# Scaling softmax weights on GpSimd instead of VectorE, with later score and value products, in a two-layer decoder trunk

## The chip, the core and the metric

The kernel runs on one core of a Trainium2 chip. The metric is device time in microseconds of one execution. Engines are named as in the profile: PE is TensorE (matrix products and transposes), PEld its weight loads, DVE is VectorE, ACT is ScalarE, POOL is GpSimd, SP issues the weight transfers. L946 is line 946 of the kernel before.

## The reference

The input is 256 tokens of width 1024 and a memory of 256 rows. Two layers follow each other; each is a half-step SwiGLU feed-forward, a token mixer, and another half-step feed-forward. The mixer of layer 0 is a chunked matrix memory (mLSTM), that of layer 1 is sliding-window attention with 16 heads of 64 channels in 2 groups, a learned sink per head, normalised queries and keys, and a partial rotation. Beside both stand four heads of 128 channels that attend to the memory (the cross heads). Both attentions end in the same way:

```
m = max(s, [sink]);  p = exp(s - m);  denom = sum(p) [+ exp(sink - m)]
out = (p / denom) @ v
```

The division p / denom is the "scaling of the softmax weights" in the title. All is float32.

## The kernel before

**Products.** A float32 product with a weight is made of three products of rounded parts: weights and activations are each split in a high and a low part (`split`, L211 on ACT rounds, L212 on DVE subtracts), and `mm3` (L225 to L227) adds high x high, high x low and low x high. A weight tile of 512 KB feeds 24 matrix products; SP fetches it, and eight split tiles of each part can be held. The small attention products are plain float32: `mmf` (L231) and `transpose` (L236).

**Order of the work.** PE and SP run in the order in which the program is written. That order is made by the class `Weave`. Its main line is the stream of projections, which yields after every four `mm3`, that is twelve matrix products. Beside it live chains, the steps of norms and heads. Each product adds a planned cost to a clock `wv.now`: 0.328 for an `mm3`, 0.107 for a transpose, 0.466 for a 256-column `mmf`; the scores of one window head add 0.97 in all. A chain yields a delay from the table `LAT` and is due when the clock has passed it. At each yield of the main line all chains that are due run one step, the oldest chain first. So a larger delay in `LAT` puts a PE step behind more projection work. The other engines take their instructions as dependencies and the compiler's ordering allow; each works in order.

**A cross head** (`cross_spawn`, L568 on). For each of two groups the query rows are normalised (`head_norm`, L368 on; its power of -1/2 at L379 is on POOL, and L381 and L383 on DVE use it), then transposed on PE (`queries`), copied by ACT with a gain, and two heads start: `cross_s` after this step, the second one `cross_m` later. A head makes scores (L231) into a bank of PSUM, DVE takes the maximum (L591), ACT the exponentials with their sums (L132 is the helper that issues them), DVE the reciprocal (L595) and the scaling (L596). After `cross_p` PE transposes the weights, ACT copies them (L603), after `cross_o` PE multiplies with the values. Cross heads 0 and 1 are those of the first group, 2 and 3 of the second.

**A window head** (`head` in `mixer_b`, L910 on; eight steps, each for two heads of the reference, numbered 0 to 7 here). Queries are normalised, rotated (`rope`, L857 to L860 on DVE), transposed and copied (ACT, out of `gcut`); the two steps of a group start `head` and `head` + `head_m` after that. A step adds a mask by a product (L920), makes scores (L925), DVE takes maxima (L929, L930) and joins the sinks (L932, L933), ACT makes exponentials, DVE sums and inverts (L941, L942) and scales in four instructions (L946): two of 128 columns, two of 256. After `head_p` PE transposes (six transposes), ACT copies (L954), after `head_o` PE multiplies with the values (L961).

The cross heads of layer 0 lie in `mixer_a`, those of layer 1 and the window heads in `mixer_b`. POOL runs the powers of the norms (L251, L379) and a few small transfers in the first feed-forward, and nothing else. Eight banks of PSUM serve all.

Of the kernel before, what the change touches and what calls it, by code (L numbers as in the profile page):

```python
# [15 lines left out]
ALU = mybir.AluOpType  # L16
# [3 lines left out]
P = 128  # L20
T = 256
# [11 lines left out]
def constants():  # L33
# [16 lines left out]

LAT = dict(pieces=1, norm=7.5, norm_b=4.8, mnorm=2.4, x0=16.0, x0_b=7.5, mkeys=7.2, cross=9.5, cross_s=1.5,
           cross_m=3.7, cross_p=8.7, cross_o=3.0, gates=20.0, scores=2.2, scores_m=8.4, num=6.9, num_r=7.5,
           keys=5.5, keys_d=7.2, query=9.0, head=1.5, head_m=2.5, head_p=9.3, head_o=4.0)


WARM = 18
# [40 lines left out]
def tile_trunk(ctx: ExitStack, tc: tile.TileContext, a, out):  # L99
    nc = tc.nc  # L100
# [27 lines left out]
    tt = nc.vector.tensor_tensor  # L128
# [21 lines left out]
    def mo():  # L150
        return mk(pb8, [P, 512], F32, "bank")
# [51 lines left out]
    pieces = [1]  # L203
# [57 lines left out]
    class Norm:  # L261
# [30 lines left out]

        def chain(self, gap=LAT['norm_b']):
            pc = mo()
# [103 lines left out]
    x0 = Norm(G_F1)  # L398

    def memory():  # L400
# [27 lines left out]
        for gi in range(2):  # L428
# [13 lines left out]
            norm.fold()  # L442
            wv.spawn(norm.chain(), LAT['mnorm'])
            gv = Group(wkv, 512, mh, ml, rows=True)
# [123 lines left out]
    def cross_spawn(gr, gi, layer, hsc, ys):  # L568
        qn = unit(F32)
        head_norm(qn, gr.ps, 2, hsc)  # L570
        cell = []

        def queries():
            ps = turn(qn)
            qT = unit(F32)
            act(qT, ps, AF.Copy, scale=gqk[:, layer:layer + 1])
            cell.append(qT)
            for m in range(2):
                wv.spawn(head(m), LAT['cross_s'] + LAT['cross_m'] * m)
            return  # L580
            yield

        def head(m):
            hd, qT = gi * 2 + m, cell[0]
            hi, lo = ys.tiles(4 + gi)
            s = mo()
            for h in range(2):
                mmf(s[:, h * T:(h + 1) * T], qT[:, m, h * P:(h + 1) * P], kT[gi][:, m], T)
            sv = halves(s)
            c = col()  # L590
            nc.vector.tensor_reduce(out=c[:, 2:4], in_=sv, axis=AX.X, op=ALU.max, negate=True)  # L591
            p = unit(F32)
            for h in range(2):
                act(p[:, h], sv[:, h], AF.Exp, bias=c[:, 2 + h:3 + h], accum_out=c[:, 4 + h:5 + h])
            nc.vector.reciprocal(c[:, 6:8], c[:, 4:6])  # L595
            tt(out=p, in0=p, in1=c[:, 6:8].unsqueeze(2).to_broadcast([P, 2, T]), op=ALU.mult)  # L596
            yield LAT['cross_p']
            tps = mo()
            for mc in range(2):
                for h in range(2):  # L600
                    transpose(tps[:, mc * T + h * P:mc * T + (h + 1) * P], p[:, h, mc * P:(mc + 1) * P])
            pT = tmp()
            nc.scalar.copy(pT, halves(tps))  # L603
            yield LAT['cross_o']
            o = mo()
            for mc in range(2):
                mmf(o[:, :T], vM[:, mc, hd * P:(hd + 1) * P], pT[:, mc], T, mc == 0, mc == 1)
            split_plain(o[:, :T], hi[:, m], lo[:, m])
            ys.done.add(8 + hd)

        wv.spawn(queries(), LAT['cross'])
# [251 lines left out]
    def mixer_b(x, nxt):  # L863
# [46 lines left out]
        def head(ch, qr):  # L910
            while wv.now < st.get("at", 1e9):
                yield 1.0
            kd, vr = st["kd"], st["vr"]
            m, j = ch % 2, ch // 4
            hi, lo = ys.tiles(ch // 2)
            c, d = col(), col()
            es = [slice(e * 64, (e + 1) * 64) for e in range(2)]
            sc = [mo(), mo()]
            for s in sc:
                nc.tensor.matmul(s[:, :384], identb, maskb[:, :384], start=True, stop=False, skip_group_check=True)  # L920
                wv.now += 0.16

            for cs, qs, ks in ((slice(0, P), slice(0, P), slice(0, P)), (slice(P, 384), slice(P, T), slice(0, T))):
                for e in range(2):
                    nc.tensor.matmul(sc[e][:, cs], qr[es[e], m, qs], kd[es[e], j, ks], start=False, stop=True,  # L925
                                     skip_group_check=True)
                wv.now += (cs.stop - cs.start) * 0.0017
            for e, s in enumerate(sc):
                nc.vector.tensor_reduce(out=c[:, e:e + 1], in_=s[:, :P], axis=AX.X, op=ALU.max, negate=True)  # L929
                nc.vector.tensor_reduce(out=c[:, 2 + e:3 + e], in_=s[:, P:384], axis=AX.X, op=ALU.max, negate=True)  # L930
            snk = nsink[:, 2 * ch:2 * ch + 2].unsqueeze(1).to_broadcast([P, 2, 2])
            tt(out=v22(c[:, 8:12]), in0=v22(c[:, 0:4]), in1=snk, op=ALU.min)  # L932
            tt(out=v22(c[:, 12:16]), in0=v22(c[:, 8:12]), in1=snk, op=ALU.subtract)  # L933
            p = [unit(F32).rearrange("p a b -> p (a b)") for _ in range(2)]
            for e in range(2):
                for h, cs in ((0, slice(0, P)), (1, slice(P, 384))):
                    i = 2 * h + e
                    act(p[e][:, cs], sc[e][:, cs], AF.Exp, bias=c[:, 8 + i:9 + i],
                        accum_out=d[:, 4 + i:5 + i])
            act(d[:, 0:4], c[:, 12:16], AF.Exp)  # L940
            tt(out=d[:, 8:12], in0=d[:, 0:4], in1=d[:, 4:8], op=ALU.add)  # L941
            nc.vector.reciprocal(d[:, 12:16], d[:, 8:12])  # L942
            for e in range(2):
                for h, cs in ((0, slice(0, P)), (1, slice(P, 384))):
                    i = 2 * h + e
                    nc.vector.tensor_scalar(p[e][:, cs], p[e][:, cs], d[:, 12 + i:13 + i], None, op0=ALU.mult)  # L946
            yield LAT['head_p']
            pTs = []
            for e in range(2):
                tps = mo()  # L950
                for i in range(3):
                    transpose(tps[:, i * P:(i + 1) * P], p[e][:, i * P:(i + 1) * P])
                pT = tmp().rearrange("p a b -> p (a b)")
                nc.scalar.copy(pT[:, :384], tps[:, :384])  # L954
                pTs.append(pT)
            yield LAT['head_o']
            o = mo()
            js = slice(j * 64, (j + 1) * 64)
            for i, cs, src in ((0, slice(0, T), slice(0, T)), (1, slice(P, T), slice(T, 384))):
                for e in range(2):  # L960
                    nc.tensor.matmul(o[es[e], cs], vr[:, i, js], pTs[e][:, src], start=i == 0, stop=i == 1,  # L961
                                     skip_group_check=True)
                wv.now += (cs.stop - cs.start) * 0.0017
            split_plain(o[:, :T], hi[:, m], lo[:, m])
            ys.done.add(ch)
# [61 lines left out]
```

## Time and profile before

| what | value |
|---|---|
| median of 3 runs | 1012.32 us (1012.27 to 1013.65) |
| the profiled execution | 1012.23 us |
| its span, first to last instruction | 1010.4 us |
| granted TensorE clock, mean | 1.000 |
| moved from memory | 180.32 MB read, 180 GB/s over the span |

The rows in the next sections are read like this. In the page's first part: engine, busy us, share of the span, number of instructions. In the chain that ended last: the share of the span in which each engine was what the end waited for. In a row of waits: who waited, for whom, us in total, how often, the longest. In a row of the timeline: start, duration (us), engine, line, operation, output<-inputs, shapes, count of like instructions drawn together, and in brackets the idle time before it and what ended that. In a row of a group: count, then busy us, mean ns of one, idle us before. In a row of stretches: bounds, length, then busy us and count for PE, PEld, DVE, ACT, POOL, then granted clock, share of the transfer engines, GB/s. Ends of matrix products are modelled, since they are pipelined: a product is shown longer than the distance to the next one.

### The profile page before, as it was taken

To read this page: it belongs to the slowest core of one execution; us is meant where nothing else is said; L and a number is where in the kernel's file an instruction comes from. 1 tells how busy PE (TensorE), PEld (TensorE's weight loads), DVE (VectorE), ACT (ScalarE), POOL (GpSimd) and SP (SyncE) were. 2 spreads that over 40 slices of the span, in tenths; PEclk is the share of its full clock that TensorE was granted. 3 is DMA by queue.
4 is the path that set the end of the run, shared out by engine and by line. 5 is a ranking of instruction groups with operands and counts; after the bars stand their busy time and mean duration, and the time that the engine had idled before them with its cause. 6 is when DMAs were issued, how large, how long until landed. Compare 5 with 4: busy or idle time off the path is not lost.

```text
span 1010.4 us, 20624 instructions
## 1 busy us (share of the span) xinstructions
PE 998.5 (99%) x8594; PEld 980.2 (97%) x8594; DVE 655.5 (65%) x1063; ACT 519.5 (51%) x764; POOL 35.7 (4%) x32
## 2 busy tenths in 40 slices
PE   8999999999999999999999999999999999999998
PEld 7999999999999999999999999999987899999998
DVE  6866665577856676665558666656787766666551
ACT  7754445446656554444445544544557754454440
POOL 1200000000001000000000000000121000000000
PEclk9999999999999999999999999999999999999999
DMA  9776656666644566665676666567541347666550
GB/s 308 242 245 200 192 180 185 199 183 179 184 139 133 167 210 195 200 189 170 192 206 205 189 191 201 173 197 198 182 131 66 100 131 220 198 189 185 188 170 21
DMA packets 173204, 182.70 MB, mean 181 GB/s; under 512 B 7124, under 2 KB 168328, under 8 KB 173112
## 3 DMA queue, kind: packets, MB, share of 16 engines
q1 hardware_dynamic: 171872, 179.60, 58.3%
q10 hardware_dynamic: 1016, 1.58, 0.5%
q8 instruction: 67, 1.10, 0.5%
q0 software_dynamic: 224, 0.22, 0.2%
q14 instruction: 25, 0.20, 0.1%
HBM read 180.32 MB, written 1.05 MB: 180 GB/s over the span
## 4 chain that ended last, share of the span: by engine, by line
PE 94%; DVE 3%; ACT 1%; DMA 1%; POOL 0%; issue 0%; SPq 0%; ACTq 0%
PE bank L225 30%; PE bank L226 30%; PE bank L227 30%; PE bank L231 2%; PE bank L236 1%; ACT u L132 1%; DVE wl L212 1%; DMA wr<-in_mem_w_kv_dram 1%; PE bank L961 1%; POOL col L379 0%; DVE col L930 0%; DVE u L383 0%; DVE col L591 0%; PE bank L925 0%; DVE u L946 0%
## 5 line engine op out<-in xcount | busy, mean ns | idle before, releaser
L212 DVE TENSOR_TENSOR wl<-wr,wh 128x1024 fp32r<-128x1024 f32 (+1 forms) x347 | 414.7, 1196 | 279.8 <-ACT wh L211 279.0
L211 ACT CAST wh<-wr 128x1024 fp32r<-128x1024 f32 (+1 forms) x347 | 356.8, 1031 | 393.1 <-PE bank L226 368.9
L225 PE MATMUL bank<-xh,wh 128*128 128x256 f32 x1544 | 429.1, 278 | 0.0
L226 PE MATMUL bank<-xl,wh 128*128 128x256 f32 x1544 | 426.8, 276 | 0.0
L227 PE MATMUL bank<-xh,wl 128*128 128x256 f32 x1544 | 426.8, 276 | 0.0
L226 PEld LDWEIGHTS bank<-xl,wh 128*128 128x128 f32 x1544 | 290.3, 188 | 0.1
L225 PEld LDWEIGHTS bank<-xh,wh 128*128 128x128 f32 x1544 | 290.0, 188 | 0.1
L227 PEld LDWEIGHTS bank<-xh,wl 128*128 128x128 f32 x1544 | 289.9, 188 | 0.0
L225 PE MATMUL bank<-u,wh 128*128 128x256 f32 x896 | 249.3, 278 | 0.0
L226 PE MATMUL bank<-u,wh 128*128 128x256 f32 x896 | 247.6, 276 | 0.0
L227 PE MATMUL bank<-u,wl 128*128 128x256 f32 x896 | 247.6, 276 | 0.0
L225 PEld LDWEIGHTS bank<-u,wh 128*128 128x128 f32 x896 | 168.2, 188 | 1.9 <-issue 1.7
L226 PEld LDWEIGHTS bank<-u,wh 128*128 128x128 f32 x896 | 168.4, 188 | 0.1
L227 PEld LDWEIGHTS bank<-u,wl 128*128 128x128 f32 x896 | 168.3, 188 | 0.0
L225 PE MATMUL bank<-wh,xh 128*128 128x256 f32 x208 | 59.7, 287 | 0.0
L226 PE MATMUL bank<-wl,xh 128*128 128x256 f32 x208 | 57.9, 278 | 0.0
L227 PE MATMUL bank<-wh,xl 128*128 128x256 f32 x208 | 57.9, 278 | 0.0
L476 DVE TENSOR_TENSOR t<-bank,rb 128x256 f32<-128x256 f32 x88 | 36.6, 420 | 7.3 <-PE bank L227 7.3
L225 PEld LDWEIGHTS bank<-wh,xh 128*128 128x128 f32 x208 | 39.1, 188 | 0.5 <-issue 0.3
L226 PEld LDWEIGHTS bank<-wl,xh 128*128 128x128 f32 x208 | 39.1, 188 | 0.1
L227 PEld LDWEIGHTS bank<-wh,xl 128*128 128x128 f32 x208 | 39.0, 187 | 0.0
L479 DVE TENSOR_TENSOR t<-t,bank 128x256 f32<-128x256 f32 x88 | 32.7, 412 | 1.8 <-ACT t L132 1.8
(171 smaller groups left out, 657.5 us busy)
## 6 DMA issues: line engine op xcount, KB each, us to landing
wr<-in_ffn_w_in_dram SPq DMA_DIRECT2D x176, 512.0 KB, 3.6
wr<-in_ffn_w_out_dram SPq DMA_DIRECT2D x80, 512.0 KB, 3.5
wr<-in_a_w_in_dram SPq DMA_DIRECT2D x28, 512.0 KB, 3.9
wr<-in_b_w_in_dram SPq DMA_DIRECT2D x14, 512.0 KB, 4.6
wr<-in_a_w_out_dram SPq DMA_DIRECT2D x12, 512.0 KB, 3.3
wr<-in_b_w_out_dram SPq DMA_DIRECT2D x12, 512.0 KB, 3.4
wr<-in_ffn_w_out_dram SPq DMA_DIRECT2D x16, 256.0 KB, 2.8
wr<-in_mem_w_kv_dram SPq DMA_DIRECT2D x7, 512.0 KB, 8.0
```

Source lines behind the costliest of these rows:

```text
L132: ins = nc.scalar.activation(*args, **kw)
L211: last[0] = nc.scalar.copy(hi[:, i * n:(i + 1) * n], src[:, i * n:(i + 1) * n])
L212: tt(out=lo[:, i * n:(i + 1) * n], in0=src[:, i * n:(i + 1) * n], in1=hi[:, i * n:(i + 1) * n].bitcast(F32), op=ALU.subtract)
L225: nc.tensor.matmul(ps, wh, xh, start=start, stop=False, skip_group_check=True)
L226: nc.tensor.matmul(ps, wh, xl, start=False, stop=False, skip_group_check=True)
L227: nc.tensor.matmul(ps, wl, xh, start=False, stop=stop, skip_group_check=True)
L231: nc.tensor.matmul(ps, lhsT, rhs, start=start, stop=stop, skip_group_check=True)
L236: nc.tensor.transpose(ps, src, ident[:k, :k])
L476: tt(out=t[:, m], in0=ps[m][:, :T], in1=x.rb, op=ALU.mult)
L479: tt(out=t[:, m], in0=t[:, m], in1=ps[m][:, T:], op=ALU.mult)
L961: nc.tensor.matmul(o[es[e], cs], vr[:, i, js], pTs[e][:, src], start=i == 0, stop=i == 1, skip_group_check=True)
```

## The change

The scaling of cross heads, one DVE instruction on 512 columns with the reciprocals broadcast, becomes two POOL instructions on 256 columns, each with its reciprocal as a column. The four scaling instructions of a window head keep their form and go from DVE to POOL. Three delays grow: `cross_s` from 1.5 to 2.5, `cross_o` from 3.0 to 3.5, `head` from 1.5 to 2.5.

```diff
-LAT = dict(pieces=1, norm=7.5, norm_b=4.8, mnorm=2.4, x0=16.0, x0_b=7.5, mkeys=7.2, cross=9.5, cross_s=1.5,
-           cross_m=3.7, cross_p=8.7, cross_o=3.0, gates=20.0, scores=2.2, scores_m=8.4, num=6.9, num_r=7.5,
-           keys=5.5, keys_d=7.2, query=9.0, head=1.5, head_m=2.5, head_p=9.3, head_o=4.0)
+LAT = dict(pieces=1, norm=7.5, norm_b=4.8, mnorm=2.4, x0=16.0, x0_b=7.5, mkeys=7.2, cross=9.5, cross_s=2.5,
+           cross_m=3.7, cross_p=8.7, cross_o=3.5, gates=20.0, scores=2.2, scores_m=8.4, num=6.9, num_r=7.5,
+           keys=5.5, keys_d=7.2, query=9.0, head=2.5, head_m=2.5, head_p=9.3, head_o=4.0)
...
-            tt(out=p, in0=p, in1=c[:, 6:8].unsqueeze(2).to_broadcast([P, 2, T]), op=ALU.mult)
+            for h in range(2):
+                nc.gpsimd.tensor_scalar(p[:, h], p[:, h], c[:, 6 + h:7 + h], None, op0=ALU.mult)
             yield LAT['cross_p']
...
-                    nc.vector.tensor_scalar(p[e][:, cs], p[e][:, cs], d[:, 12 + i:13 + i], None, op0=ALU.mult)
+                    nc.gpsimd.tensor_scalar(p[e][:, cs], p[e][:, cs], d[:, 12 + i:13 + i], None, op0=ALU.mult)
             yield LAT['head_p']
```

## Prediction

> **What bounds the kernel now.** I began with the page: busy time of each engine, then the chain that ended last.
>
> ```profile
> span 1010.4 us, 20624 instructions
> ...
> PE 998.5 (99%) x8594; PEld 980.2 (97%) x8594; DVE 655.5 (65%) x1063; ACT 519.5 (51%) x764; POOL 35.7 (4%) x32
> ...
> PE 94%; DVE 3%; ACT 1%; DMA 1%; POOL 0%; issue 0%; SPq 0%; ACTq 0%
> ```
>
> TensorE (PE) is the bound and holds 94% of the chain; only what makes it idle can be won. GpSimd (POOL) is nearly free. The table of stretches shows where PE idles around the change: the first mixer, a stretch of pure feed-forward, and the second mixer.
>
> ```profile
> 230.00:358.00 128.00, 128.00 (x1060) 125.99 (x1059) 88.85 (x167) 76.88 (x136) 7.03 (x6) 1.00 0.53 158
> 358.00:545.00 187.00, 187.00 (x1648) 187.00 (x1648) 119.43 (x172) 89.79 (x108) 2.24 (x2) 1.00 0.65 197
> ...
> 720.00:840.00 120.00, 114.67 (x942) 103.78 (x942) 88.50 (x235) 72.74 (x176) 15.35 (x9) 1.00 0.39 121
> ```
>
> The first number after the length is PE's busy time. The first mixer loses nothing, the second loses 5.3 us. The second row also gives the pace: 187.00/1648 = 0.1135 us a matmul, so the twelve between two yields of a projection, a "slot" below, are 1.36 us. PE's waits in the second mixer:
>
> ```profile
> PE bank L231 <- ACT u L132: 1.5, 1, 1.5
> PE bank L925 <- ACT u L132: 1.4, 1, 1.4
> PE bank L231 <- ACT t L603: 1.1, 1, 1.1
> PE bank L920 <- DVE u L383: 0.7, 1, 0.7
> PE bank L961 <- ACT u L132: 0.4, 1, 0.4
> PE bank L920 <- ACT t L954: 0.2, 1, 0.2
> ```
>
> They add up to 5.3 us, the whole loss, and are all that this change can give back. The first three lie before 762 us; the timeline shows them with what released them:
>
> ```profile
> 741.74 0.69 ACT L132 ACTIVATE u<-bank,gqk 128x512 f32<-128x512 f32 x1
> ...
> 742.47 0.73 PEld L231 LDWEIGHTS bank<-kT,u 128*128 128x128 f32 x4 [1.66 <-ACT u L132]
> 742.47 1.13 PE L231 MATMUL bank<-kT,u 128*128 128x256 f32 x4 [1.45 <-ACT u L132]
> ...
> 750.45 0.57 ACT L603 COPY t<-bank 128x512 f32<-128x512 f32 x1
> ...
> 751.08 1.13 PE L231 MATMUL bank<-t,vM 128*128 128x256 f32 x4 [1.05 <-ACT t L603]
> ...
> 754.23 0.93 PE L925 MATMUL bank<-u,u 64*128 64x128 f32 x8
> ...
> 760.29 0.74 ACT L132 ACTIVATE u<-bank,gcut 128x512 f32<-128x512 f32 x1
> ...
> 761.09 0.93 PE L925 MATMUL bank<-u,u 64*128 64x128 f32 x8 [1.40 <-ACT u L132]
> ```
>
> Each time PE reaches a score or value product before ScalarE has made its copy: scores of cross head 2, values of cross head 0, scores of window head 2. These are just the three kinds whose delays grow: cross_s, cross_o, head.
>
> **The delays.** The planner runs due chains at yields; a slot is 4 x 0.328 = 1.31 of its time. Set its clock to 0 at the end of the first cross turn. Now: two slots 2.62, scores 0 end 3.56, a slot 4.87, second turn 5.30, scores 1 (due 1.5 + 3.7 = 5.2) end 6.23, a slot 7.54, scores 2 (due 5.30 + 1.5 = 6.8). After: scores 1 are due at 6.2, so a slot comes first (6.61), end 7.54, a slot 8.85, scores 2 (due 7.8). Between second turn and scores 2 stand two slots for one: 1.36 us of work inside a 1.45 us wait. Gain **1.35 us**.
>
> Values of cross head 0: due 3.0 after their transposes, met today after scores 3 (0.93), a slot and the next transposes (0.43), 2.67. After, 3.5 is not met before scores of window head 0, which then stand due and go first (0.97 planned). From the end of scores 3 the copy took until 751.02. The same distance is then covered by about 1.3 us of products for 0.6 us of transposes, and VectorE comes earlier to the max that ScalarE's queue waited for. I take 0.85 of the 1.05 us as gone, from 0 to all.
>
> Window head 2: by the same clock its scores start 4.03 after the end of head 1's scores today and 5.77 after; the difference is 1.74 planned, over a slot. Today the copy ended 761.03 - 755.16 = 5.9 us after those scores, and PE came there 1.40 too early. With 1.7 us more work it comes late enough. Gain **1.40 us**.
>
> The price is that window head 0's scores come nearer to their own copy:
>
> ```profile
> 746.27 1.04 PE L236 MATMUL bank<-con,u 128*128 128x128 f32 x8
> ...
> 747.72 0.71 ACT L132 ACTIVATE u<-bank,gcut 128x512 f32<-128x512 f32 x1
> ```
>
> The copy ended 2.15 us after its transposes began; after, 0.43 + 0.43 + 0.93 + 1.31 = 3.1 us of work stand between, but with one slot fewer ahead of the turn. I take 0.1 us of new wait, at most 0.6. No chain issues a DMA and the projections keep their order, so SP's queue is untouched; POOL's DMAs all lie in the first feed-forward.
>
> **The scaling.** VectorE's cost in this stretch, by group:
>
> ```profile
> L946 DVE TENSOR_SCALAR u<-u,col 128x128 f32<-128x128 f32 (+1 forms) x32 | 8.0, 315 | 0.1
> ...
> L596 DVE TENSOR_TENSOR u<-u,col 128x512 f32<-128x512 f32 x4 | 2.7, 687 | 0.1
> ```
>
> So 10.7 us leave VectorE: 8.0/8 = 1.0 a window head, 0.69 a cross head. VectorE does not bound, so this counts only where it feeds ScalarE ahead of a PE wait: it is the help counted at the second wait. The same instructions on POOL are nowhere in the trace. The nearest rows are its powers:
>
> ```profile
> 727.76 1.01 POOL L379 TENSOR_TENSOR col<-col,mhalf 128x4 f32<-128x4 f32 x1 [4.19 <-DVE col L377]
> ...
> 771.96 2.48 POOL L379 TENSOR_TENSOR col<-col,mhalf 128x8 f32<-128x8 f32 x1 [20.88 <-DVE col L377]
> 779.09 1.64 POOL L379 TENSOR_TENSOR col<-col,mhalf 128x8 f32<-128x8 f32 x1 [4.66 <-DVE col L377]
> ```
>
> Four columns 1.01, eight 1.64: 0.16 a column on a fixed 0.38. The lower end is VectorE's own 0.32 an instruction, the upper 2.48, a power's longest here. I take the fixed part and 1 ns a column (VectorE's 687 ns for 512, rounded up): 0.51 and 0.64, an estimate, so **2.3 us a window head**, 1.3 a cross head, nearer the lower end because a multiplication is what VectorE does there.
>
> The 2.48 stands against 1.64 for the same shape. What else ran:
>
> ```profile
> 771.72 1.22 DVE L212 TENSOR_TENSOR wl<-wr,wh 128x1024 fp32r<-128x1024 f32 x1
> ```
>
> The long power started inside VectorE's weight split and ended 1.50 us after it; a wait of 0.84 is to be reckoned with. Beside this: the Trainium skill, "SBUF — State Buffer", section "Who interferes with whom", says that a VectorE instruction with two SBUF inputs and a GpSimd instruction that reads SBUF exclude each other for a whole instruction, whichever starts second waiting. The trace agrees for POOL's side (2.48 against 1.64); VectorE's waiting side no row here shows. By that rule VectorE would not be relieved of all 10.7 us: that is the second rival.
>
> A window head's weights are thus ready 2.3 - 1.0 + 0.84 = 2.1 us later. The cover is PE's distance to their transposes:
>
> ```profile
> 742.23 0.68 DVE L596 TENSOR_TENSOR u<-u,col 128x512 f32<-128x512 f32 x1
> ...
> 745.27 0.68 DVE L596 TENSOR_TENSOR u<-u,col 128x512 f32<-128x512 f32 x1
> ...
> 749.43 0.60 PE L236 MATMUL bank<-con,u 128*128 128x128 f32 x4
> ...
> 758.93 1.01 DVE L946 TENSOR_SCALAR u<-u,col 128x128 f32<-128x128 f32 x4
> ...
> 788.33 1.01 DVE L946 TENSOR_SCALAR u<-u,col 128x128 f32<-128x128 f32 x4
> ...
> 793.17 0.88 PE L236 MATMUL bank<-con,u 128*128 128x128 f32 x6
> ...
> 806.66 0.82 PE L236 MATMUL bank<-con,u 128*128 128x128 f32 x6
> ```
>
> Window head 4 has 793.17 - 789.34 = 3.8 us, cross head 1 749.43 - 745.95 = 3.5, cross head 0 about 3.8 to the second half of the eight at 746.27, of which the lifted first wait takes 1.4. Each is more than its 2.1 or 1.5. In the first mixer the cover is larger:
>
> ```profile
> 264.00 0.69 DVE L596 TENSOR_TENSOR u<-u,col 128x512 f32<-128x512 f32 x1
> ...
> 270.11 0.60 PE L236 MATMUL bank<-con,u 128*128 128x128 f32 x4
> ```
>
> The new wait is POOL's on the reciprocal. Queued behind it stand the next head's weights and the next query norm's power, which VectorE's line 381 needs. The one that matters follows window head 3:
>
> ```profile
> 769.82 1.01 DVE L946 TENSOR_SCALAR u<-u,col 128x128 f32<-128x128 f32 x4
> ...
> 777.20 0.60 PE L236 MATMUL bank<-con,u 128*128 128x128 f32 x4
> ```
>
> With 2.3 us POOL is done by 772.1, when the power would run anyway (771.96); the turn at 777.20 then stays. For this and for changed bank reuse I add 0.3 us. The three later waits (1.3 us) I leave.
>
> **Sum:** -1.35 - 0.85 - 1.40 + 0.1 + 0.3 = -3.2 us on the profiled execution's own 1012.23 us (span 1010.4 and 1.8 outside it, untouched): 1009.0. The median is 0.09 above that execution, so I forecast **1009.1 us**.
>
> **The rivals.** *POOL too slow (slower).* Place: transposes of the window weights. Head 0's weights begin at 758.93; 32 instructions of p us and two powers (4.1) must end by 806.66 plus the 3.6 us lifted, so p = (51.3 - 4.1)/32 = 1.48 us is where the gain is used up; window head 4 by itself makes PE wait from (793.17 - 788.33)/4 = 1.2. Powers of 1.01 to 2.48 speak for it, the small fixed part of 0.38 against. At p = 1.6 it adds 0.12 x 32 = 3.9 us: **1016.2 us**; at 2.48, 1044.
>
> *The waits only move (same).* VectorE is held up by POOL as POOL is by it, so maxima and copies come no earlier, and waits two and three reappear a slot later. Only the first wait's 1.35 goes, less 0.3 to 0.6: **1011.4 us**. For it: the 0.84 above. Against: cover of 1.7 planned at the third wait needs no help from VectorE.
>
> *All six go (faster).* VectorE, rid of 1.0 us a head, serves the three later waits earlier too. PE's rows understate a wait a little (its weight load has 1.66 where the product has 1.45); with 0.1 for each of six it is 1012.3 - 5.3 - 0.6 = **1006.4 us**.
>
> *It does nothing:* excluded for the order, by the clock above.
>
> **Chances.** Forecast 0.50, all six go 0.10, only moved 0.22, POOL too slow 0.18. A measurement of this kernel can tell about 0.2%, 2 us, from no change: faster is below 1010.3, same up to 1014.3. Of the forecast's half, 0.05 ends above 1010.3. So faster 0.55, same 0.27, slower 0.18. The range runs from 1006.2 (all waits gone, nothing paid) to 1014.8 (p just past 1.48), leaving out most of the slow rival.
>
> As to line rate: the Trainium skill, "GPSIMD Engine Reference", section 4.1, puts one-input work on GpSimd at roughly VectorE's line rate. No run here shows it yet; by it the weights would be no later at all and the sum 0.3 us lower, 1008.8.
>
> **What would show it.** Right: waits at 742 and 761 gone, the one at 751 under 0.3; POOL's multiplications near 0.5 to 0.7 us, longer beside the split of weights; no PE wait on POOL. Wrong: transposes (L236) waiting for POOL; VectorE's splits longer than 1.22 us; new waits on ScalarE's copies a slot later; or the power after window head 3 later than 774.4 and its turn with it.

## The result and the profile after

The changed kernel takes **1016.27 us** (median of 6 runs, 1016.01 to 1017.73; the kernel before on the same chip 1012.3), a ratio of 1.004 with the 95% interval [1.0027, 1.0053]. It is slower by 4 us, where 3.2 us less were forecast, and lies above the range. The profiled execution took 1016.08 us. Two lines of its page (span, and the shares of the chain that ended last), then the rows of the two mixers from the table of stretches. Each stretch runs from PE's last sums of squares ahead of a mixer (the rows L231 `bank<-ones,acc`) to the next ones behind it, so that it can be laid over the same stretch of another kernel; the columns are those of the earlier table.

```profile
span 1014.3 us, 20676 instructions
...
PE 92%; DVE 3%; POOL 2%; ACT 2%; issue 1%; DMA 1%; SPq 0%; POOLq 0%; ACTq 0%; DVEq 0%
```

The same two mixers before:

```profile
223.81:357.75 133.94, 133.94 (x1110) 131.93 (x1109) 91.63 (x172) 78.86 (x137) 7.75 (x7) 1.00 0.55 162
719.04:833.89 114.85, 109.52 (x898) 98.63 (x897) 85.08 (x234) 71.40 (x175) 13.82 (x8) 1.00 0.37 113
```

And after:

```profile
223.64:358.20 134.56, 134.22 (x1110) 131.85 (x1109) 89.49 (x168) 78.87 (x137) 15.11 (x15) 1.00 0.54 161
719.48:837.79 118.31, 110.28 (x899) 98.54 (x898) 76.39 (x198) 71.26 (x175) 48.32 (x48) 1.00 0.35 110
```

VectorE is indeed relieved, by 8.7 us in the second mixer (85.08 to 76.39), GpSimd has 34.5 us more, and GpSimd, nowhere before, holds 2% of the chain. The first mixer is 0.62 us longer, the second 3.46; PE's idle time in the second grew from 5.3 to 8.0, and the other 0.8 us is PE longer busy (109.52 to 110.28). The sum of 4.1 is the whole loss: outside the two stretches both executions spend 737.0 us between PE's very first sums of squares and the end. These first sums stand at 24.3 to 24.7 us in most traces and at 25.9 to 26.2 in four (e2, e12, e14 and e16 below); in just these four the granted clock was 0.50 for 3.4 us between 13 and 18 us. Such executions take some 1.6 us longer (1013.8 for 1012.1, the kernel before), so the experiments below are read by the lengths of these two stretches first, called A (before 133.95, after 134.56) and B (before 114.86, after 118.30). Both come from one profiled execution of each kernel; a second trace of the changed kernel gives 134.56 and 118.20.

PE's waits in the second mixer, after:

```profile
PE bank L921 <- DVE u L383: 2.5, 2, 1.3
PE bank L236 <- POOL u L947: 1.6, 1, 1.6
PE bank L225 <- DVE u L383: 1.1, 1, 1.1
PE bank L231 <- ACT u L132: 1.0, 1, 1.0
PE bank L926 <- ACT u L132: 1.0, 2, 0.7
PE bank L236 <- DVE u L861: 0.4, 1, 0.4
PE bank L231 <- ACT t L604: 0.4, 1, 0.4
```

Hardly a row of before is left: 8.0 us of waits, other ones. The three that the change was to lift are lifted, as the timeline of after shows at the same three products (lines behind 596 have moved by one: L925 is now L926):

```profile
742.94 1.13 PE L231 MATMUL bank<-kT,u 128*128 128x256 f32 x4
...
749.25 0.93 PE L926 MATMUL bank<-u,u 64*128 64x128 f32 x8 [0.31 <-ACT u L132]
750.11 1.13 PE L231 MATMUL bank<-t,vM 128*128 128x256 f32 x4
...
762.49 0.93 PE L926 MATMUL bank<-u,u 64*128 64x128 f32 x8
```

Scores of cross head 2, values of cross head 0 and scores of window head 2 have no wait behind them; window head 0's scores have 0.31, inside the forecast bound of 0.6. So the 3.9 us were won, and 3.9 + 4.1 = 8.0 lost elsewhere. (That the waits left in the second mixer also come to 8.0 is chance: some of these stood there before, and the first mixer and PE's longer busy time are in the other sum.)

**GpSimd's price.** Its groups on the whole kernel:

```profile
L597 POOL TENSOR_SCALAR u<-u,col 128x256 f32<-128x256 f32 x16 | 16.4, 1037 | 19.6 <-DVE col L595 12.6 <-DVE acol L722 7.1
L947 POOL TENSOR_SCALAR u<-u,col 128x256 f32<-128x256 f32 x16 | 15.5, 971 | 0.0
...
L947 POOL TENSOR_SCALAR u<-u,col 128x128 f32<-128x128 f32 x16 | 11.3, 706 | 16.0 <-DVE col L943 12.2 <-DVE col L934 2.7 <-ACT u L132 1.2
```

A window head's four instructions take 2 x 0.706 + 2 x 0.971 = 3.35 us, a cross head's two 2.07; 2.3 and 1.3 were forecast. All 48 cost 43.2 us against 8 x 2.3 + 8 x 1.3 = 28.8.

**GpSimd's queue.** GpSimd works in order, and the power of the query norm that VectorE's line 381 needs now stands behind heads' weights. The timeline around the third power (GpSimd, VectorE, PE):

```profile
747.12 2.73 POOL L597 TENSOR_SCALAR u<-u,col 128x256 f32<-128x256 f32 x2 [2.64 <-DVE col L595]
...
747.58 0.51 DVE L377 TENSOR_SCALAR col<-col,qsc 128x4 f32<-128x4 f32 x2
...
749.83 1.66 POOL L379 TENSOR_TENSOR col<-col,mhalf 128x8 f32<-128x8 f32 x1
...
751.52 0.58 DVE L381 TENSOR_SCALAR col<-col,qsc 128x4 f32<-128x4 f32 x2 [2.38 <-POOL col L379]
752.14 0.69 DVE L383 TENSOR_TENSOR u<-bank,col 128x512 f32<-128x512 f32 x1
...
752.88 0.48 PE L921 MATMUL bank<-maskb,identb 128*128 128x384 bf16 x2 [1.21 <-DVE u L383]
```

The power's input was there at 747.58 + 0.51 = 748.09, its start is at 749.83: 1.74 us in the queue behind a cross head's weights (2.73 for two instructions, beside a weight split on VectorE). Line 383 reads a bank of PSUM and frees it; it ends at 752.83, and at 752.88 PE, which needs a bank, goes on after 1.21 us. The same again behind window heads 2 and 3:

```profile
771.86 0.66 DVE L377 TENSOR_SCALAR col<-col,qsc 128x4 f32<-128x4 f32 x2
...
774.26 1.67 POOL L379 TENSOR_TENSOR col<-col,mhalf 128x8 f32<-128x8 f32 x1
...
775.97 0.36 DVE L381 TENSOR_SCALAR col<-col,qsc 128x4 f32<-128x4 f32 x2 [3.45 <-POOL col L379]
...
776.36 0.69 DVE L383 TENSOR_TENSOR u<-bank,col 128x512 f32<-128x512 f32 x1
...
777.20 0.35 PE L225 MATMUL bank<-u,wh 128*128 128x256 f32 x1 [1.13 <-DVE u L383]
```

Input at 772.52, start at 774.26, again 1.74 late; VectorE sat idle 3.45 us for it, and PE waits 1.13 for the bank.

Not all of this is the queue's. From input to end the two powers take 3.40 and 3.41 us here. In the kernel with the new delays and all scaling on VectorE (e2 below) they start at once and take 2.6 and 1.8, the first being long because it runs beside a weight split (2.54). So the queue makes them 0.8 and 1.6 us later, and e2 too has a PE wait of 0.99 us for a bank of line 383 near the first of them.

**A row to read with care** is the one wait on GpSimd's weights, 1.6 us. Its timeline:

```profile
801.81 3.72 POOL L947 TENSOR_SCALAR u<-u,col 128x128 f32<-128x128 f32 x4 [2.60 <-DVE col L943]
802.05 1.22 DVE L212 TENSOR_TENSOR wl<-wr,wh 128x1024 fp32r<-128x1024 f32 x1
...
802.33 0.55 PE L236 MATMUL bank<-con,u 128*128 128x128 f32 x3
...
803.18 0.15 DVE L933 TENSOR_TENSOR col<-col,nsink 128x4 f32<-128x4 f32 x1
...
804.14 0.20 ACT L132 ACTIVATION_READ_ACCUMULATOR u<-bank,col 128x1 f32 x1
...
804.44 0.52 PE L236 MATMUL bank<-con,u 128*128 128x128 f32 x3 [1.57 <-POOL u L947]
```

The transposes at 802.33 and 804.44 are the two halves of window head 5, whose weights GpSimd had finished by 799.2 in the group before (it starts at 795.64 and takes 3.57). The group named, at 801.81, is head 6's. These transposes also need a bank. Window head 7's exponentials release one at 804.34, 0.1 us before PE goes on, and they were late because VectorE joined that head's sinks (803.18) only behind a weight split (802.05 to 803.27). So by the times this wait is for a bank, and no wait on the weights themselves is left in this kernel. That reading rests on the times; the rows don't name the bank.

### The profile page after: what moved, and what is told of

Same layout as the page of the kernel before. It is cut to its first block, busy times and chain, and to the rows that moved or that the text cites. A ratio compares the mean times of both kernels' runs of the same rounds, so it can differ in the third digit from the quotient of the medians.

```text
span 1014.3 us, 20676 instructions
## 1 busy us (share of the span) xinstructions
PE 999.0 (98%) x8594; PEld 979.9 (97%) x8594; DVE 645.0 (64%) x1023; ACT 519.8 (51%) x764; POOL 76.5 (8%) x80
## 3 DMA queue, kind: packets, MB, share of 16 engines
HBM read 180.32 MB, written 1.05 MB: 179 GB/s over the span
## 4 chain that ended last, share of the span: by engine, by line
PE 92%; DVE 3%; POOL 2%; ACT 2%; issue 1%; DMA 1%; SPq 0%; POOLq 0%; ACTq 0%; DVEq 0%
PE bank L226 30%; PE bank L225 30%; PE bank L227 29%; PE bank L231 2%; ACT u L132 1%; DVE wl L212 1%; PE bank L236 1%; POOL col L379 1%; DMA wr<-in_mem_w_kv_dram 1%; POOL u L947 1%; ACT wh L211 0%; POOL u L597 0%; PE bank L926 0%; PE bank L962 0%; DVE col L931 0%
## 5 line engine op out<-in xcount | busy, mean ns | idle before, releaser
L211 ACT CAST wh<-wr 128x1024 fp32r<-128x1024 f32 (+1 forms) x347 | 356.9, 1031 | 392.4 <-PE bank L226 369.9
L251 POOL TENSOR_TENSOR rc<-col,mhalf 128x2 f32<-128x2 f32 x7 | 6.8, 964 | 629.7 <-DVE col L250 451.2
```

Source lines behind the costliest of these rows:

```text
L211: last[0] = nc.scalar.copy(hi[:, i * n:(i + 1) * n], src[:, i * n:(i + 1) * n])
L251: nc.gpsimd.tensor_tensor(out=dst, in0=c[:, :n], in1=mhalf[:, :n], op=ALU.pow)
```

## The experiments

Each run is given with its median, the ratio to the kernel before with its 95% interval, and A and B.

**The clock in the second mixer.** Not every B can be compared as it stands. In seven traces (e3, e7, e9, e11, e15, e17, e18) the granted clock was 0.50 for 3.4 us inside the second mixer, in e3 and e15 for 6.8; in before, after and all others it was 1.00 there. Two stretches of e18 show it, the 3.4 us before and the 3.4 at half clock (the clock is the third number from the end):

```profile
748.70:752.10 3.40, 1.53 (x8) 0.87 (x6) 2.17 (x8) 2.47 (x7) 1.64 (x1) 1.00 0.40 154
752.20:755.60 3.40, 3.40 (x18) 1.81 (x18) 3.33 (x10) 0.63 (x2) 0.00 (x0) 0.51 0.01 2
```

PE had waited, and was busy for 1.53 of the 3.4 us before. In the other six traces it was busy for 0.9 to 1.6 of the 3.4 us before. The clock's records are whole multiples of 3.4 us; where PE was busy for 1.8 us or more of such a piece of the second mixer at full clock, no half clock followed in any trace. So by these traces waits of PE that fall into one piece can cost a second time, up to 1.7 us (half of 3.4) a piece, and since the pieces lie differently in each execution, not in every one. The tables mark with * a B that holds such a stretch, and give the times of the executions whose mean granted clock was 0.999 or 1.000 ("full clock", number of executions in brackets). The kernel before takes about 1012.1 us at full clock, the changed kernel 1016.0 to 1016.6.

**GpSimd alone, delays alone.** The kernel after with the old `LAT` (e1), and with the scaling back on VectorE (e2).

> The scaling on POOL alone, with the three delays of before. Queue theory (POOL's multiplications, 0.61 us for 128 columns and 0.93 for 256, stand in front of the query norms' powers, and VectorE, which works in order, waits for these powers): 1015 to 1020 us, with PE's old waits of 1.0 to 1.5 us back beside the new ones on line 383. Rival (the later scores and values do the harm by another order of steps and banks): 1011 to 1013 us.

> The three delays alone, the scaling on VectorE as before. Queue theory: the forecast's gain of 1.35 + 0.85 + 1.40 less 0.1 is there when POOL does not take it away, 1008 to 1010 us, no PE wait over 1 us in the second mixer but the one on line 383. Rival (the delays do the harm): 1014 us or more, with PE waits on line 383 near the mask products as in the changed kernel.

| kernel | us | ratio | A | B | full clock |
|---|---|---|---|---|---|
| e1_pool_only | 1014.95 | 1.0018 [1.0004, 1.0033] | 133.95 | 116.13 | 1013.3 to 1013.5 (2) |
| e2_delays_only | 1015.14 | 1.003 [1.002, 1.0041] | 134.59 | 117.26 | 1014.9 to 1015.1 (4) |

Both parts cost by themselves: the delays 0.6 + 2.4, GpSimd 1.3, nearly all of it in the second mixer. Together they cost 0.6 + 3.4, a little less than the sum. In e1 two of the three old waits are still there (1.47 and 1.43 us); the one at the values of cross head 0 is gone, with VectorE relieved. Its new waits are not on line 383, where the queue theory put them, but for banks that ScalarE holds (L132 1.3 us, L955 1.2), and the time falls between the two forecasts. In e2 the three are gone as they are in after, and the waits on PE in the second mixer are these:

```profile
PE bank L925 <- ACT u L132: 2.6, 2, 1.4
PE bank L920 <- DVE u L383: 1.3, 1, 1.3
PE bank L231 <- ACT t L603: 1.2, 1, 1.2
PE bank L236 <- DVE u L383: 1.0, 1, 1.0
...
```

The kinds are the old ones (a query copy, a value copy, a bank that line 383 holds), at other heads.

**Each delay alone**, on the kernel before.

```diff
 e7:  cross_s=1.5  ->  cross_s=2.5
 e8:  cross_o=3.0  ->  cross_o=3.5
 e9:  head=1.5     ->  head=2.5
```

> The kernel before with cross_s 2.5 alone. Theory A (cross_s does the harm of the delays: cross scores a slot later bring window head 0's scores ahead of two older steps and their query copy behind more of ScalarE's queue): most of the delays' 2.9 us, 1014 to 1015.5 us; the wait at cross head 2's scores gone, one over 1 us at window head 0's scores. Theory B (the harm is head's or cross_o's): 1010.5 to 1012 us.

> The kernel before with cross_o 3.5 alone. Theory A: 1011 to 1012.5 us, the wait of 1.05 us at cross head 0's values shorter, the two others as before. Theory B: 1014 us or more.

> The kernel before with head 2.5 alone. Theory A: 1010 to 1012 us, the wait of 1.40 us at window head 2's scores gone or shorter. Theory B: 1014 us or more.

| kernel | us | ratio | A | B | full clock |
|---|---|---|---|---|---|
| e7_cross_s_only | 1015.44 | 1.0031 [1.0019, 1.0043] | 134.56 | 117.34* | 1014.07 (1) |
| e8_cross_o_only | 1011.99 | 0.9999 [0.9982, 1.0016] | 134.13 | 114.46 | 1011.8 to 1012.0 (7) |
| e9_head_only | 1018.6 | 1.0061 [1.0044, 1.0077] | 133.95 | 120.44* | none |

`cross_s` alone gives most of the loss of the three delays: at full clock, in one execution, 2.0 of 2.9 us, of which 0.6 are in A. `cross_o` moves nothing that can be measured (B 0.4 shorter, A 0.2 longer). `head` alone is the worst of all: PE waits 9.4 us in the second mixer, against 5.3 before, and the half clock comes right behind the longest of these waits (2.5 us). Yet with all three delays (e2) PE waits only 7.2 us: the delays don't add up, since each one changes what is due at the next yield.

**Which cross head carries it.** Raising `cross_s` shifts all four cross heads. e17 shifts only the second head of each group, e18 only the first one.

```diff
 e17: cross_s=1.5, cross_m=3.7  ->  cross_s=1.5, cross_m=4.7
 e18: cross_s=1.5, cross_m=3.7  ->  cross_s=2.5, cross_m=2.7
```

> The kernel before with cross_m raised by 1.0 (to 4.7) and cross_s left, so that only the second cross head of each group (1 and 3) makes its scores later, as it does with cross_s raised; cross heads 0 and 2 keep their due times. cross_s alone took 117.34 us in the second mixer and 134.56 in the first, before 114.86 and 133.95. Theory (the later scores of cross head 1, with its maximum, exponentials and the query copies behind them, carry the loss): 116.5 us or more in the second mixer and 134.3 or more in the first. Rival (the loss comes with the later scores of cross head 2, or with the order in general): under 115.7 in the second and 134.0 in the first.

> The kernel before with cross_s raised by 1.0 (to 2.5) and cross_m lowered by 1.0 (to 2.7), so that cross heads 1 and 3 keep their due times and the scores of cross head 2 alone stand a slot later, which lifts the wait at 742 (1.45 us). Theory (cross head 1's later scores carry the loss of cross_s): this kernel keeps the gain without the loss, 113.5 to 114.9 us in the second mixer and 133.95 in the first, about 1011 to 1012.3 in all. Rival (any shift of these steps moves the waits to other places): 115.5 us or more in the second mixer.

| kernel | us | ratio | A | B | full clock |
|---|---|---|---|---|---|
| e17_second_heads_later | 1015.62 | 1.003 [1.0012, 1.0048] | 133.94 | 118.20* | 1014.32 (1) |
| e18_first_heads_later | 1012.96 | 1.0012 [0.9989, 1.0035] | 134.09 | 115.42* | 1012.8 to 1013.0 (4) |

In B the theory holds: the second heads alone cost 3.3 us in the trace and 2.2 at full clock (one execution), more than the 1.4 that `cross_s` as a whole costs there; the first heads cost 0.6 and 0.8. In A it fails: neither reaches the 0.6 us of `cross_s`. And e18 keeps no gain: it falls between the two forecasts, closer to the rival. How the loss in B begins shows the timeline of e17, ahead of its half clock:

```profile
743.44 1.23 DVE L212 TENSOR_TENSOR wl<-wr,wh 128x1024 fp32r<-128x1024 f32 x1 [0.48 <-ACT wh L211]
744.58 1.28 DVE L591 TENSOR_REDUCE col<-bank 128x2 f32<-128x512 f32 x2
745.30 0.47 ACT L132 ACTIVATE u<-bank,col 128x256 f32<-128x256 f32 x1 [1.89 <-DVE col L591]
...
747.60 1.06 ACT L211 CAST wh<-wr 128x1024 fp32r<-128x1024 f32 x1
...
749.57 1.04 ACT L211 CAST wh<-wr 128x1024 fp32r<-128x1024 f32 x1 [0.91 <-ACT wh L211]
...
750.52 0.68 ACT L132 ACTIVATE u<-bank,gcut 128x512 f32<-128x512 f32 x1
...
751.25 0.93 PE L925 MATMUL bank<-u,u 64*128 64x128 f32 x8 [1.43 <-ACT u L132]
```

against the kernel before, whose second mixer begins at the same time within 0.05 us:

```profile
742.83 0.68 DVE L591 TENSOR_REDUCE col<-bank 128x2 f32<-128x512 f32 x1
743.43 1.21 DVE L212 TENSOR_TENSOR wl<-wr,wh 128x1024 fp32r<-128x1024 f32 x1
743.54 0.47 ACT L132 ACTIVATE u<-bank,col 128x256 f32<-128x256 f32 x1 [0.19 <-DVE col L591]
```

A slot later on PE, cross head 1's maximum (L591) comes behind the weight split on VectorE instead of ahead of it: 744.58 for 742.83. Its exponentials follow 1.76 us later on ScalarE, and the weight rounding behind them (L211, 747.60) still 0.8 us later than before (746.78). Then ScalarE idles 0.91 us and takes one more rounding ahead of the query copy out of `gcut`, where before it took the copy at once. So this copy, which began at 747.72 before, begins at 750.52, 2.8 us later: 0.8 by the maximum, 2.0 by ScalarE's changed order, for which the rows give no reason. Window head 0's scores meet it too early, by 1.43 us. A delay that puts PE 1.36 us later has thus put ScalarE's copy 2.8 us later. e2 has two roundings there too, and the same wait of 1.43; in the changed kernel only one stands ahead of the copy, and PE waits 0.31.

This is not yet the whole loss. The wait of 1.05 us that stood at the values of cross head 0 is gone in e17, so this meeting costs 0.4 us net. More comes from two waits for banks, 2.09 us at 768.11 (line 246) and 2.08 at 784.18 (line 383), while the old wait at 761 is gone. How these two follow from the shift is not shown.

e18 shows the other half, what becomes of a wait that is lifted cleanly:

```profile
742.72 1.13 PE L231 MATMUL bank<-kT,u 128*128 128x256 f32 x4
...
748.91 0.68 DVE L591 TENSOR_REDUCE col<-bank 128x2 f32<-128x512 f32 x1
749.63 0.47 ACT L132 ACTIVATE u<-bank,col 128x256 f32<-128x256 f32 x1 [1.66 <-DVE col L591]
...
750.09 0.58 ACT L603 COPY t<-bank 128x512 f32<-128x512 f32 x1
...
750.72 1.13 PE L231 MATMUL bank<-t,vM 128*128 128x256 f32 x4 [1.87 <-ACT t L603]
```

The 1.45 us ahead of cross head 2's scores are gone, and at the next meeting, the values of cross head 0, PE waits 1.87 instead of 1.05: the copy L603 stands on ScalarE behind an exponential that waits for VectorE. Counted from the start of B it ends 0.6 us earlier than before, where PE comes 1.4 us earlier. (The old wait at 761 is missing in this trace, behind the half clock.)

**Holding window head 0 back.** My first theory of the delays was that window head 0's scores had moved ahead of two other products, too near to their own query copy.

```diff
-                wv.spawn(head(2 * gi + m, qr), LAT['head'] + LAT['head_m'] * m)
+                wv.spawn(head(2 * gi + m, qr), LAT['head'] + LAT['head_m'] * m + (1.0 if gi == 0 else 0.0))
```

> The three new delays with all scaling on VectorE, and window heads 0 and 1 held back by a further 1.0, so that by the planner's clock window head 0's scores come behind the values of cross head 0 and the transposes of cross head 1 again. The delays alone took 117.26 us in the second mixer, against 114.86 before. Theory (the delays cost because window head 0's scores are moved ahead, towards their own query copy, and take a bank that the transposes then lack): the waits at 752 (1.5 us) and 755 (1.0) go, the second mixer takes 114.6 to 115.6 us, about 1013.2 in all with the 0.6 of the first mixer. Rival (the delays cost because cross head 1's later scores put its maximum and all that follows on VectorE and ScalarE behind other work): query copies and value copies stay late, the second mixer stays above 116.5 us.

> The changed kernel with window heads 0 and 1 held back by a further 1.0 likewise. The changed kernel took 118.30 us in the second mixer. If the costs of the delays and of GpSimd add up, it falls as much as the kernel with the delays alone does by the same hold: by some 2 us to about 116.2 where the theory of the order holds, by under 0.8 where the rival does. If the cost of GpSimd's queue is what decides in this order (the power of the query norm behind two window heads' weights), the waits on VectorE's line 383 stay (3.6 us) and it stays above 117.5.

e15_hold_group0 took 1018.13 us, 1.0055 [1.0027, 1.0082], A 134.59, B 119.97*, and 1015.28 in one execution at full clock, about as much as without the hold (e2): the theory falls. Window head 0's wait of 1.5 us did go, with 0.7 at its mask product in its place, but others came: 2.0 us for a bank that line 383 holds at 770, and 2.3 for banks that line 246 holds at 786 to 788. e16_after_hold isn't what its expectation says: its kernel is the changed kernel, unaltered. As such it gives 1016.23 us, 1.0028 [1.001, 1.0046], A 134.56, B 118.20, a repeat of the result; the hold in the changed kernel was not tried.

**The queue on GpSimd.** The changed kernel with the weights ahead of the two late powers back on VectorE: cross head 1 of layer 1, and window heads 2 and 3.

```diff
-                nc.gpsimd.tensor_scalar(p[:, h], p[:, h], c[:, 6 + h:7 + h], None, op0=ALU.mult)
+                eng = nc.vector if (layer, hd) == (1, 1) else nc.gpsimd
+                eng.tensor_scalar(p[:, h], p[:, h], c[:, 6 + h:7 + h], None, op0=ALU.mult)
...
+                    (nc.vector if ch in (2, 3) else nc.gpsimd).tensor_scalar(p[e][:, cs], ...)
```

> The changed kernel with the scaling of only three heads of the second mixer back on VectorE: cross head 1, which stands in front of the second query norm's power, and window heads 2 and 3, in front of the third's. Five of eight window heads' and seven of eight cross heads' POOL work stays. Queue theory: the powers start within 0.3 us of their input, 1011 to 1013.5 us, what is left being the transposes of window head 4 that wait for POOL. Rivals (contention for memory ports, or POOL's share as such): a loss in proportion, 1015 us or more.

It took 1015.64 us, 1.0028 [1.0017, 1.004], A 134.59, B 118.44*. No weights stand in front of the two powers any more, and the waits that go back to line 383 fell from 3.6 to 0.7 us. In the trace B is no shorter, for a new wait of 3.1 us heads the list, at the value copy of cross head 0 again (L605), behind an exponential that waits 3.03 us for VectorE's maximum; and with it, at 752.7, begin 6.8 us at half clock. The one execution at full clock took 1013.62 us; the five others lie 1.3 to 1.5 us above it at a mean clock of 0.998 and 2.5 to 2.9 above it at 0.997. So at full clock three heads back on VectorE win some 2.5 us against the changed kernel. That speaks for the queue theory, whose range it misses by 0.1, and against a loss in proportion; but it rests on one execution, and VectorE's order changes with the edit too.

**GpSimd's work without the relief of VectorE.** The scaling stays on VectorE; GpSimd multiplies a constant of the same shapes by the same reciprocals, into a tile that nobody reads. On the new delays (e6), on the old ones (e11), and on the old ones with powers of four columns, three a window head and two a cross head, for the multiplications (e12).

```diff
+                    nc.gpsimd.tensor_scalar(idle2[:, cs], con[:, cs], d[:, 12 + i:13 + i], None, op0=ALU.mult)
...
+                nc.gpsimd.tensor_tensor(out=idle2, in0=d[:, 12:16], in1=mhalf[:, 0:4], op=ALU.pow)
```

> The new delays with the scaling on VectorE, and beside it on POOL, for each head, the same instructions on a constant with the same reciprocals into a tile that nobody reads: nothing in the program waits for POOL but the powers behind them. Queue theory: the powers start late again, most of the loss against the delays alone comes back, 1012.5 to 1016 us. Rival (the loss is that the weights themselves come later to their transposes): within 1 us of the delays alone.

> The kernel before (old delays, scaling on VectorE), with the same multiplications on a constant on POOL beside it, into a tile that nobody reads. Queue theory: the third query norm's power waits 1 to 2 us behind window heads 2 and 3 and the second mixer takes 116.5 to 118.5 us against 114.86. Rival (POOL costs only where weights wait for it): 114.9 to 115.3.

> As the twin with old delays, but POOL's idle work is powers of four columns (1.01 us each, three a window head, two a cross head): the same time on POOL and next to no reads. Queue theory: within 0.7 us of the twin. Rival (memory ports shared with VectorE): clearly nearer to the kernel before, within 0.5 us of its second mixer of 114.86.

| kernel | us | ratio | A | B | full clock |
|---|---|---|---|---|---|
| e6_twin_on_pool | 1018.98 | 1.008 [1.0058, 1.0102] | 134.56 | 120.33 | 1018.0 to 1018.1 (3), 1025.5 (1) |
| e11_twin_old_delays | 1016.91 | 1.0036 [1.0023, 1.005] | 133.89 | 119.77* | 1015.7 to 1016.6 (3) |
| e12_small_twin_old_delays | 1021.1 | 1.0095 [1.0058, 1.0132] | 134.24 | 117.21 | 1020.5 to 1021.2 (3) |

Work on GpSimd that nobody reads costs 3.1 us of B on the new delays and, at full clock, 3.6 to 4.5 us in all on the old; small powers, which read nearly nothing, 2.4 of B. The real move costs 1.0 and 1.3. So GpSimd in this place costs some 3 to 4.5 us and VectorE's relief gives some 2 to 3 back. e6 and e11 cost more than both of their forecasts, and e12 lies between its two. How the cost divides between the queue and what the multiplications do to VectorE isn't separated: in e12 the powers also come at other times. e12's total can't be used: in its trace (1029.24 us) the first feed-forward is 6.4 us longer and the last 6.3, where the edit does nothing. There PE has no waits, but its products follow each other in 0.117 us for 0.113 at a granted clock of 1.00, and I found no reason.

**The changed kernel without the costly delay.** e10 is the kernel after with `cross_s=1.5`.

> The changed kernel with cross_s back at 1.5, so POOL scales and cross_o and head stay at their new values. Theory A: as the scaling alone on POOL or a little better, 1012.5 to 1015 us, and the first mixer back at 133.9 us. Theory B: as the changed kernel, 1016 us or more.

1014.78 us, 1.0018 [1.0005, 1.0032], A 134.13, B 117.25, and 1014.7 to 1014.8 at full clock (7): 0.4 us of A and 1.0 of B are won back, less than the 2.0 that `cross_s` alone costs. In this kernel PE does wait for weights: the transposes from 776.28 to 777.77 wait 1.1 us in three pieces for GpSimd, which begins these weights only at 773.72.

**GpSimd where no power follows.** Only window heads 4 to 7 scaled on GpSimd, all else as before (e13), and with `cross_o` 0.5 more in layer 1 (e14).

```diff
-                    nc.vector.tensor_scalar(p[e][:, cs], p[e][:, cs], d[:, 12 + i:13 + i], None, op0=ALU.mult)
+                    (nc.gpsimd if ch >= 4 else nc.vector).tensor_scalar(p[e][:, cs], ...)
...
-            yield LAT['cross_o']
+            yield LAT['cross_o'] + 0.5 * layer
```

> The kernel before with the scaling of window heads 4 to 7 alone on POOL; no power follows them in the mixer. Queue theory: no harm, second mixer 114.2 to 115.0 us, 1011.5 to 1012.5. Rival (weights come too late to their transposes, 3.1 us and more on POOL against 1.0): a PE wait on POOL over 0.5 us, 1012.8 us or more.

> A try at a faster version: window heads 4 to 7 on POOL and cross_o 3.5 in the second layer only. If the two add up, the second mixer takes 113.9 to 114.6 us and the time is 1011 to 1012 us; if the new order meets other waits, 1012.5 us or more.

| kernel | us | ratio | A | B | full clock |
|---|---|---|---|---|---|
| e13_last_four_pool | 1012.23 | 1.0002 [0.9986, 1.0019] | 133.89 | 114.38 | 1011.7 to 1012.3 (7), 1018.6 (1) |
| e14_last_four_pool_cross_o | 1013.21 | 0.9996 [0.9984, 1.0009] | 133.95 | 113.97 | 1011.3 to 1011.8 (4) |

The same multiplications at about the same price cost nothing there. B is 0.5 us shorter than before and the rest of the execution 0.5 longer (a longer tail behind PE's last product). PE's waits in e13 are the old ones less the one at line 961, and none is on GpSimd. So a slow multiplication by itself isn't what costs here. That its place ahead of a power is what costs elsewhere fits e3, but the heads differ in more than that. e14 has the shortest B of all, 0.9 us under before; at full clock its median is 0.65 us under that of the kernel before (1012.09 in the same set of runs), but its ratio doesn't differ from 1: no version here beats both kernels by more than can be measured.

## Why the prediction was wrong

**The bound and the waits.** Right: PE is the bound, only its 5.3 us of waits could be won, and the three waits lie where the delays act. The clock arithmetic was right too: all three are gone in after and in e2. Window head 0's new wait is 0.31 us in after, where 0.1 was taken and 0.6 allowed, but 1.43 in e2. The help of VectorE that was put into the second term is borne out: in e1, with the old delays, this wait is gone.

**The delays: the step that failed.** The prediction booked -1.35 - 0.85 - 1.40 and, as "the price", 0.1 us. Measured by themselves the delays are +0.6 in the first mixer and +2.4 in the second, where -3.5 stood. It took a lifted wait for a gain, with VectorE and ScalarE keeping their order and times. They don't. `cross_s` also put cross head 1's scores a slot later, and the prediction's clock had them (6.61 to 7.54 for 5.30 to 6.23), but counted only the slot that this put ahead of cross head 2. It did not follow the scores to VectorE, where their maximum then stands behind a split of 1.2 us, nor on to ScalarE, where in e17 and e2 one more rounding then stands ahead of the query copy, 2.8 us later in e17. Also the order that it gave ("scores of window head 0, which then stand due and go first") was right and its effect not followed: PE's products of other heads change places, and with them the bank each waits for. e17 and e2 show such new waits in B; not every one of them is traced to its cause. Why `cross_s` costs 0.6 us in A is open: there PE waits 0.3 us for VectorE where it waited for nothing, and neither half of the shift does that alone.

**The rival "the waits only move".** It gave 1011.4 on the ground that maxima and copies come no earlier. That is near to what e18 shows, one wait lifted (1.45) and the next grown (1.05 to 1.87), with copies 0.6 us earlier where PE is 1.4. It erred in the size: new waits can be longer than those they replace.

**The scaling.** The price was 0.51 and 0.64 us against 0.706 and 0.971 measured, free of VectorE's splits 0.605 and 0.925. The slope was wrong: 1 ns a column was taken, (0.925 - 0.605)/128 = 2.5 ns are measured; the fixed part, 0.38 taken, is 0.29. (Nor is 2.48 a power's longest in the trace of before: one at 737.26 takes 2.54.) The cover of 3.5 to 3.8 us held all the same, and the one row that names GpSimd's weights is, by its times, a bank. The term for the power was too small: "With 2.3 us POOL is done by 772.1, when the power would run anyway" was the one place that the prediction looked at, and there the power came 1.74 us late and PE waited 1.13; the second place, the power behind cross head 1's weights, it didn't price (1.21). The trace thus has 2.3 us of waits where 0.3 stood. Not all of them are the queue's, since e2 waits 0.99 for a bank of line 383 without it; but e3 at full clock wins some 2.5 us by taking the weights away from these two places.

**The rival "POOL too slow"** gave 1016.2 us, the measured time, by chance, for a reason that the runs don't bear out: it asked for 1.6 us an instruction and for transposes that wait for weights, while the mean is 0.7 to 1.0, and 3.0 of the 4.1 us come with the delays alone. The Trainium skill's "roughly line-rate" for one-input work ("GPSIMD Engine Reference", section 4.1), by which the sum was to be 0.3 lower, this trace doesn't bear out: 0.706 and 0.971 us against VectorE's 0.315 mean for the same instructions.

**What would show it.** Of the named signs the lifted waits came, the power after window head 3 came at 774.26, just short of the 774.4 named, three of VectorE's splits took 1.36 to 1.45 us for 1.22, one row names GpSimd at the transposes (for a bank, by its times), and "new waits on ScalarE's copies a slot later" came in full in e2 (1.43 and 1.15 us) and in small in after (0.31 and 0.37).

## What to carry to other kernels

When an engine with an order fixed ahead is made to arrive later at a wait, follow the moved step on through every engine that feeds the next meeting, above all past the long instructions it may now queue behind (here a weight split of 1.2 us): a shift of 1.36 us on PE came out as 2.8 us on ScalarE. Before work goes to an idle engine, list what small instruction already runs there and who waits for it: its delay can cost more than the moved work's own duration, and where nothing followed (e13) the same work was free. A wait row that names an engine is to be checked against that engine's own times. And before stretches of two traces are compared, the granted clock inside them is to be looked at: here seven traces hold 3.4 or 6.8 us at half clock, behind PE's own waits.

## What the runs showed of the chip

A multiplication of float32 by a column takes GpSimd 0.605 us for 128x128 and 0.925 for 128x256 when VectorE's weight splits are away; VectorE needs 0.28 and 0.35. Beside a split GpSimd's instruction stretches: the cross head's two at 747.12 took 2.73 us for 1.85. VectorE's split is stretched too, but less. Most splits beside GpSimd's work stay at 1.22 us; those that started 0.74 us or more before a multiplication ended are longer, here two of them:

```profile
762.88 1.42 DVE L212 TENSOR_TENSOR wl<-wr,wh 128x1024 fp32r<-128x1024 f32 x1 [0.52 <-ACT wh L211]
...
791.71 1.36 DVE L212 TENSOR_TENSOR wl<-wr,wh 128x1024 fp32r<-128x1024 f32 x1
```

A third, at 276.50, takes 1.45. All three end 0.62 or 0.63 us after that multiplication. The rule of the Trainium skill that the prediction weighed ("SBUF — State Buffer", "Who interferes with whom"), by which the second to start waits for the whole instruction, is seen on GpSimd's side, where multiplications begun inside a split (748.04, 755.68, 802.39) end 0.79 us after it; on VectorE's side these rows show a wait of 0.1 to 0.2 us, a part of it.

The granted TensorE clock was 0.50 for pieces of 3.4 us, and in the second mixers of these traces this began only behind a piece in which PE was busy for 0.9 to 1.6 us.
